# A two-layer decoder trunk on one core: rows of x loaded once, and the first half-step's instructions in a fixed order

## The chip, the core and the metric

The program runs on one core of one Trainium2 chip. The metric is the device time of one execution in microseconds. The kernel before takes 971.33 us (median of 3 runs, 970.76 to 971.44). A core has five engines with a queue of instructions each, which start in their order: TensorE (PE, with its weight loads as PEld), VectorE (DVE), ScalarE (ACT), GpSimd (POOL) and SyncE (SP, which here issues loads). They wait for each other by semaphores only.

## The reference, cut to what matters

```python
def rmsnorm(x, g):                      # x: 256 tokens x 1024, float32
    y = x * lax.rsqrt(jnp.mean(x * x, axis=-1, keepdims=True) + EPS)
    return y * g

def swiglu(x, w_gate, w_up, w_down):    # 1024 -> 2816 -> 1024
    return (jax.nn.silu(x @ w_gate) * (x @ w_up)) @ w_down

for l in range(2):
    x = x + 0.5 * swiglu(rmsnorm(x, ffn1_norm[l]), ...)      # the first half-step is this one, l = 0
    x = x + mixer(rmsnorm(x, mix_norm[l]))                   # conv and windowed attention, or block attention
    x = x + memory_cross_attention(rmsnorm(x, xa_norm[l]), mem_n, ...)
    x = x + 0.5 * swiglu(rmsnorm(x, ffn2_norm[l]), ...)
return rmsnorm(x, final_norm)
```

The change touches the start of the program and the first half-step up to about its sixth pair of gate and up columns; the arithmetic is the same.

## The kernel before, in words

x lies transposed, as eight rows of tiles `x[:, k]` (128 features by 256 tokens). Every product takes float32 apart into a high and a low part: `x2.hi` and `x2.lo` for activations, `whi` and `wlo` for weights. For one 128x128 weight tile, `mm` issues two matmuls, `whi` against both parts of x (512 columns, L391) and `wlo` against the high part (256 columns, L392). Together they are called a pair of matmuls below.

Weights come in the order of use. `Stream` loads chunks of 16 tiles (1 MB) into four `raw` buffers on SP's queue, and splits them in blocks of 8 tiles: ACT writes `whi` (L127), then DVE writes `wlo` (L128), into five buffers each. `_due_to` names how many blocks ahead of use a block may be split (`AHEAD_BLOCKS`, 4), `fill` and `flush` do it. The first 32 tiles are special: `load_first` loads one piece for each row k (L87), which holds row k of x and the four gate tiles that go with it, so x reaches the first matmuls with their weights; x is loaded a second time, whole, to the place where it stays (L1092, after a one-element copy by POOL that delays it).

The half-step computes 22 columns f of gate and of up. `gates` does the gates of f = 0 to 3 at once, row by row, as x comes in: blocks 0 to 3. Then `gate_up` does up of f = 0 to 3 (blocks 4 to 7), and from f = 4 on a gate block and an up block in turn (f = 4 is blocks 8 and 9, f = 5 is 10 and 11). A finished column is joined from its two halves in PSUM (`join`: ACT L401, then DVE L402).

1/rms is not needed for the matmuls. It comes beside them: squares on ACT and their sums on DVE (L327 to L338), a sum over features on PE (L354), the power -1/2 on POOL (L359), a transpose that spreads it over the partitions (PE L365) and a copy to `rbc` (ACT L367). Columns that are finished before that wait in a list (`n.waiting`). `evac` then takes a column f through gate times `rbc` (DVE L525), silu (ACT L526), times up (DVE L528), high part (ACT L459) and low part (DVE L460).

The order on each engine is made in two steps. `Order.run` calls the pieces by planned PE times (`pe.after(delay, ...)`), and a scheduler then may move instructions on each engine, except those that are given to `keep_in_program_order` (by `ws.pin` for splits).

Of the kernel before, what the change touches and what calls it, by code (L numbers as in the profile page):

```python
# [53 lines left out]
class Stream:  # L54
# [23 lines left out]
    def load_first(self):  # L78

        rows = []  # L80
        for k in range(KT):
            if k % 2 == 0:
                t = self.raw[k // 2] = self._raw()
            o = k % 2 * STEP
            cuts = (0, S + P, STEP) if k == 0 else (0, STEP)
# [69 lines left out]
    def take(self, name, layer, row, col, n=1, rows=1):  # L155

        i = len(self.order)
        for k in range(n):  # L160
            at = k % 2 * P
            self.order.append((name, layer, row, col + k * P, 1) if n == 1 else
                              (name, layer, row, col + 2 * at + k // 2, 2) if rows == 1 else
                              (name, layer, row + at, col + k // 2, 2))
        b, o = divmod(i, BLK)
        assert o + n <= BLK and n in (1, 4)
        self._load_to(self.chunk_of(b)[0] + 1 + self.AHEAD_CHUNKS)
        self._due_to(b + 1 + self.AHEAD_BLOCKS)
        while self.n_split <= b:
            self.fill()  # L170
        if self.part and self.n_split == b + 1 and o + n > BLK // 2:
            self.step()
        hi, lo = self.split[b]
        return hi[:, o * P:(o + n) * P], lo[:, o * P:(o + n) * P]


class Order:
# [3 lines left out]
    def __init__(self):  # L181
        self.t = 0.0
        self.tasks = []
        self.n = 0

# [57 lines left out]
def build(nc, tc, ctx, a):  # L243
# [31 lines left out]
    first_rows = ws.load_first()  # L275
# [45 lines left out]
    def squares(n, k, stream):  # L321

        if k < KT - 2:
# [3 lines left out]
            nc.scalar.activation(sq, stream[:, k - 1:k + 1].rearrange("p k s -> p (k s)"), AF.Square)  # L327
            if k == 1:
                n.acc = sq
            else:  # L330
                nc.vector.tensor_tensor(n.acc, n.acc, sq, op=ALU.add)
            if k == KT - 3:
                two, n.acc = n.acc, act.tile([P, S], F32, name="sqacc", bufs=2)
                nc.vector.tensor_tensor(n.acc, two[:, :S], two[:, S:], op=ALU.add)
# [5 lines left out]
    def norm_scale(n, delay=2300, unpin=False, wide=True, turn=True):  # L340
# [5 lines left out]
        def sums():  # L346
            pt = tr_tile()
            ms = act.tile([P, 2], F32, name="ms", bufs=2)
            for t in range(2):
                part = n.acc[:, t * P:(t + 1) * P]  # L350
                if turn:
                    nc.tensor.transpose(pt[:, t * P:(t + 1) * P], part, ident)
                else:
                    nc.tensor.matmul(pt[:, t:t + 1], part, ones, start=True, stop=True)  # L354
            if turn:
                nc.vector.tensor_reduce(ms, halves(pt[:, :S]), axis=AX.X, op=ALU.add)
            nc.vector.tensor_scalar(ms, ms if turn else pt[:, :2], 1.0 / D, EPS, op0=ALU.mult, op1=ALU.add)
            n.rcol = act.tile([P, 2], F32, name="rcolm" if n.keep else "rcol", bufs=1 if n.keep else 2)
            nc.gpsimd.tensor_tensor(n.rcol, ms, mhalf, op=ALU.pow)  # L359
            pe.after(*((2200, spread, 120) if wide else (1400, known, 0)))  # L360

        def spread():
            pt = tr_tile()
            for t in range(2):
                nc.tensor.transpose(pt[:, t * P:(t + 1) * P], n.rcol[:, t:t + 1].to_broadcast([P, P]), ident)  # L365
            n.rbc = act.tile([P, S], F32, name="rbcm" if n.keep else "rbc", bufs=1 if n.keep else 2)
            nc.scalar.activation(n.rbc, pt[:, :S], AF.Copy)  # L367
            known()

        def known():  # L370
            n.ready = True
            ws.fine = False
            if unpin:
                ws.pin = None
            for fn in n.waiting:
                fn()
# [11 lines left out]
    def mm(ps, w, x2, start, stop):  # L388


        nc.tensor.matmul(ps, w[0], x2.both, start=start, stop=False)  # L391
        nc.tensor.matmul(ps[:, :S], w[1], x2.high, start=False, stop=stop)  # L392
# [7 lines left out]
    def join(out, ps):  # L400
        nc.scalar.activation(halves(out), unpaired(ps[:, S:]), AF.Copy)  # L401
        nc.vector.tensor_tensor(halves(out), unpaired(ps[:, :S]), halves(out), op=ALU.add)  # L402
# [88 lines left out]
    def ffn(which, layer, n, nxt, first=False, last=False):  # L491
# [3 lines left out]
        def gates():  # L495
# [3 lines left out]
            for k in range(KT):  # L499
                for f in range(SIDE):  # L500
                    w = ws.take(f"{which}_w_gate", layer, k * P, f * P)
                    mm(cur[f, 0], w, n.x[k], k == 0, k == KT - 1)
            for f in range(SIDE):
                cur[f, 0] = join(w1(), cur[f, 0])

        def gate_up(f, part, ks):
            def go():
# [15 lines left out]
        def evac(f, g, u):  # L523

            nc.vector.tensor_tensor(g, g, n.rbc, op=ALU.mult)  # L525
# [5 lines left out]
            ws.flush()  # L531

# [74 lines left out]
        if first:  # L607
            for k in range(KT):
                pe.after(12000 + 1800 * (k // 2), lambda k=k: squares(n, k, x), 0)
        norm_scale(n, 18900 if first else 2300, unpin=True, turn=not first)  # L610
# [471 lines left out]
    for k in range(KT):  # L1082
# [6 lines left out]
        if k == KT // 2 - 1:  # L1089
# [122 lines left out]
```

## Time and profile before

| what | value |
|---|---|
| median of 3 runs | 971.33 us |
| the profiled execution's own time | 971.57 us |
| its span, first to last instruction | 969.8 us |
| PE busy | 959.2 us, 99% |
| DVE busy, ACT busy | 760.2 us (78%), 614.1 us (63%) |
| granted TensorE clock, mean | 0.999 |

The span leaves 1.8 us of the execution outside. Busy times are sums over the whole span; a busy PE is one with a matmul in its pipeline. The clock column of the page is in tenths of full speed and shows 9 (90% or more) in all 40 slices.

### The profile page before, as it was taken

How to read it: one execution, taken by the hardware profiler on the slowest of the kernel's cores; microseconds unless marked ns; L12 is line 12 of the kernel's file. 1: busy time of each engine (PE TensorE's matmuls, PEld its weight loads, DVE VectorE, ACT ScalarE, POOL GpSimd, SP SyncE). 2: the span in 40 equal slices, each digit the busy share in tenths (PEclk: the TensorE clock that was granted, in tenths of full speed). 3: DMA queues.
4: the chain of work that ended last, by engine and by line, in shares of the span. 5: the costliest groups of instructions: out<-in, count | busy, mean ns of one | idle time of the engine just before them, and what ended most of it. 6: DMA issues, size and time to landing. Idle time of an engine off the chain costs nothing.

```text
span 969.8 us, 16906 instructions
## 1 busy us (share of the span) xinstructions
PE 959.2 (99%) x6536; PEld 899.6 (93%) x6536; DVE 760.2 (78%) x1361; ACT 614.1 (63%) x1144; POOL 55.7 (6%) x95
## 2 busy tenths in 40 slices
PE   9999999999999999999999999999999999999997
PEld 8899999999999999999999999999999999999896
DVE  7988867898878888876778878677878789887663
ACT  7767655697657766665556666556785667666541
POOL 0410000001000000000000000000000003400011
PEclk9999999999999999999999999999999999999999
DMA  9797556555536656556555565565645346775631
GB/s 372 272 333 284 187 205 211 170 189 196 190 111 211 231 191 215 194 198 215 184 208 198 193 218 184 207 208 183 223 147 189 116 167 242 243 253 187 212 131 44
DMA packets 29921, 196.73 MB, mean 203 GB/s; under 512 B 3848, under 2 KB 4872, under 8 KB 7184
## 3 DMA queue, kind: packets, MB, share of 16 engines
q1 hardware_dynamic: 27072, 187.44, 55.5%
q0 software_dynamic: 2192, 7.37, 2.2%
q8 instruction: 51, 0.84, 0.3%
q10 hardware_dynamic: 576, 0.83, 0.2%
q14 instruction: 30, 0.25, 0.1%
HBM read 193.51 MB, written 5.27 MB: 205 GB/s over the span
## 4 chain that ended last, share of the span: by engine, by line
PE 97%; DVE 1%; DMA 1%; ACT 0%; issue 0%; SPq 0%; POOLq 0%; DVEq 0%; ACTq 0%
PE acc L391 41%; PE acc L392 21%; PE acc L397 7%; PE acc L398 7%; PE acc L396 7%; PE acc L574 1%; PE acc L573 1%; PE acc L572 1%; PE acc L918 1%; PE acc L916 1%; PE acc L917 1%; DMA raw<-in_w 1%; PE sc L572 0%; PE sc L574 0%; PE sc L573 0%; DVE wlo L128 0%
## 5 line engine op out<-in xcount | busy, mean ns | idle before, releaser
L127 ACT ACTIVATE whi<-raw 128x1024 fp32r<-128x1024 f32 (+2 forms) x377 | 369.2, 986 | 274.0 <-PE acc L391 133.3
L128 DVE TENSOR_TENSOR wlo<-raw,whi 128x1024 fp32r<-128x1024 f32 (+2 forms) x377 | 426.6, 1136 | 144.7 <-ACT whi L127 141.6
L391 PE MATMUL acc<-x,whi 128*128 128x512 f32 x1392 | 457.4, 383 | 0.9 <-DVE w L402 0.5
L392 PE MATMUL acc<-x,wlo 128*128 128x256 f32 x1392 | 377.4, 273 | 0.6 <-DVE wlo L128 0.6
L391 PEld LDWEIGHTS acc<-x,whi 128*128 128x128 f32 x1392 | 262.2, 189 | 37.4 <-ACT whi L127 1.1
L392 PEld LDWEIGHTS acc<-x,wlo 128*128 128x128 f32 x1392 | 267.2, 192 | 1.9 <-DVE wlo L128 0.9
L391 PE MATMUL acc<-h,whi 128*128 128x512 f32 x462 | 151.3, 382 | 0.0
L392 PE MATMUL acc<-h,wlo 128*128 128x256 f32 x462 | 125.4, 273 | 0.0
L391 PEld LDWEIGHTS acc<-h,whi 128*128 128x128 f32 x462 | 87.1, 189 | 12.0
L392 PEld LDWEIGHTS acc<-h,wlo 128*128 128x128 f32 x462 | 88.7, 192 | 0.2
L396 PE MATMUL acc<-h,whi 128*128 128x256 f32 x322 | 87.2, 279 | 1.6 <-ACT h L459 1.6
L397 PE MATMUL acc<-h,whi 128*128 128x256 f32 x322 | 88.1, 276 | 0.3 <-DVE h L460 0.3
L398 PE MATMUL acc<-h,wlo 128*128 128x256 f32 x322 | 87.8, 275 | 0.0
L402 DVE TENSOR_TENSOR w<-acc,w 128x256 f32<-128x256 f32 x195 | 81.1, 416 | 3.8 <-ACT w L401 3.5
L398 PE MATMUL acc<-x,wlo 128*128 128x256 f32 x304 | 83.9, 278 | 0.0
L397 PE MATMUL acc<-x,whi 128*128 128x256 f32 x304 | 83.8, 277 | 0.0
L396 PE MATMUL acc<-x,whi 128*128 128x256 f32 x304 | 83.4, 279 | 0.0
L401 ACT ACTIVATE w<-acc 128x256 f32<-128x256 f32 x195 | 71.9, 369 | 10.0 <-PE acc L392 9.8
L396 PEld LDWEIGHTS acc<-h,whi 128*128 128x128 f32 x322 | 60.5, 192 | 2.6 <-ACT h L459 2.0
L397 PEld LDWEIGHTS acc<-h,whi 128*128 128x128 f32 x322 | 61.7, 192 | 0.8 <-DVE h L460 0.7
L398 PEld LDWEIGHTS acc<-h,wlo 128*128 128x128 f32 x322 | 61.7, 192 | 0.1
L397 PEld LDWEIGHTS acc<-x,whi 128*128 128x128 f32 x304 | 58.2, 192 | 0.2
(211 smaller groups left out, 1180.7 us busy)
## 6 DMA issues: line engine op xcount, KB each, us to landing
raw<-in_w SPq DMA_DIRECT2D x171, 1024.0 KB, 5.0
dists<-line POOLq DMA_DIRECT2D x2, 1536.0 KB, 13.3
raw<-in_memT SPq DMA_DIRECT2D x3, 1024.0 KB, 5.1
raw<-in_w SPq DMA_DIRECT2D x6, 384.0 KB, 6.8
bias<-dists POOLq DMA_DIRECT2D x2, 1024.0 KB, 11.3
x<-in_xT SPq DMA_DIRECT2D x1, 1024.0 KB, 7.6
tok<-q POOLq DMA_DIRECT2D x32, 32.0 KB, 3.5
bias<-tok POOLq DMA_DIRECT2D x1, 1024.0 KB, 7.7
```

The costliest lines, as they stand in the source:

```text
L127: for ins in (self.nc.scalar.activation(hi[:, at], src, AF.Copy), self.nc.vector.tensor_tensor(lo[:, at], src, hi[:, at].bitcast(F32), op= ...
L128: self.nc.vector.tensor_tensor(lo[:, at], src, hi[:, at].bitcast(F32), op=ALU.subtract)):
L391: nc.tensor.matmul(ps, w[0], x2.both, start=start, stop=False)
L392: nc.tensor.matmul(ps[:, :S], w[1], x2.high, start=False, stop=stop)
L396: nc.tensor.matmul(ps[:, :S], w[0], x2.high, start=start, stop=False)
L397: nc.tensor.matmul(ps[:, :S], w[0], x2.low, start=False, stop=False)
L398: nc.tensor.matmul(ps[:, :S], w[1], x2.high, start=False, stop=stop)
L401: nc.scalar.activation(halves(out), unpaired(ps[:, S:]), AF.Copy)
L402: nc.vector.tensor_tensor(halves(out), unpaired(ps[:, :S]), halves(out), op=ALU.add)
L572: nc.tensor.matmul(ps, hh, wh, start=f == 0, stop=False)
L573: nc.tensor.matmul(ps, hh, wl, start=False, stop=False)
L574: nc.tensor.matmul(ps, hl, wh, start=False, stop=f == FT - 1)
```

## The change

It has five parts.

1. `load_first` loads rows 2 to 7 of x in pairs straight to where x stays, and the weights of these rows by themselves. Rows 0 and 1 still come with their weights, and once more at the end by a load of their own. The whole load of x and POOL's copy in front of it are gone.
2. From the end of the gates (`pe.kept`) until the pairs that waited for 1/rms are done, the matmuls, joins, squares, sums and splits are all given to `keep_in_program_order`.
3. Meanwhile the stream splits 2 blocks ahead of use instead of 4 (`ws.ahead`).
4. All squares go pairwise, and they stand around the joins of the gates; 1/rms is planned at 16500 instead of 18900, its spreading 2900 after it instead of 2200.
5. The waiting columns are started one each 2000 of planned time, and each goes through `evac_steps`, three steps that are 1300 apart, instead of all at once through `evac`.

The diff, cut to its core (wrapping single instructions in `keep` is shown once):

```diff
+        self.ahead = 2
...
+            if k % 2 == 0 and k > 0:
+                self.nc.sync.dma_start(x[:, k:k + 2], xT[:, k:k + 2])
+            cuts = (0, S + P, STEP) if k == 0 else (0, STEP) if k == 1 else (S, STEP)
             for i, j in zip(cuts, cuts[1:]):
                 (self.nc.scalar if k == 1 else self.nc.sync).dma_start(t[:, o + i:o + j], self.first[k][:, i:j])
-            rows.append(t[:, o:o + S])
+            rows.append(t[:, o:o + S] if k < 2 else x[:, k])
+        self.nc.sync.dma_start(x[:, :2], xT[:, :2])
...
-        self._due_to(b + 1 + self.AHEAD_BLOCKS)
+        self._due_to(b + 1 + self.ahead)
...
+    def keep(ins):
+        return tc.keep_in_program_order(ins) if pe.kept else ins
...
-        nc.tensor.matmul(ps, w[0], x2.both, start=start, stop=False)
+        keep(nc.tensor.matmul(ps, w[0], x2.both, start=start, stop=False))
...
-            for fn in n.waiting:
-                fn()
+            n.pending = len(n.waiting)
+            for i, fn in enumerate(n.waiting):
+                pe.after(i * 2000, fn, 0) if pe.kept else fn()
...
+            pe.kept, ws.pin = True, tc.keep_in_program_order
+            ws.fill()
+            for k in range(4):
+                squares(n, k, x, KT)
+            ws.fill()
             for f in range(SIDE):
                 cur[f, 0] = join(w1(), cur[f, 0])
+            ws._due_to(FIRST // BLK + 3)
+            ws.fill()
+            for k in range(4, KT):
+                squares(n, k, x, KT)
...
+        def evac_steps(f, g, u):
+            def gate():
+                keep(nc.vector.tensor_tensor(g, g, n.rbc, op=ALU.mult))
+                keep(nc.scalar.activation(g, g, AF.Silu))
+                pe.after(1300, high, 0)
+            def high():
+                keep(nc.vector.tensor_tensor(u, g, u, op=ALU.mult))
+                h[f] = h_tile()
+                keep(nc.scalar.activation(h[f].hi, halves(u), AF.Copy))
+                pe.after(1300, low, 0)
+            def low():
+                keep(nc.vector.tensor_tensor(h[f].lo, halves(u), h[f].hi.bitcast(F32), op=ALU.subtract))
+                n.pending -= 1
+                if not n.pending:
+                    pe.kept, ws.pin, ws.ahead = False, None, ws.AHEAD_BLOCKS
+            gate()
...
-        norm_scale(n, 18900 if first else 2300, unpin=True, turn=not first)
+        norm_scale(n, 16500 if first else 2300, unpin=True, turn=not first)
...
-            nc.gpsimd.tensor_copy(x[:, 0, :1], block[1][:, :1].bitcast(F32))
-            nc.sync.dma_start(x, a["xT"])
```

What this does to the engines' queues is seen at three places. The first is SP's queue at the program's start, where `raw` is a buffer for weights (384, 768 and 512 columns are pieces of the first 32 tiles, 2048 is a chunk) and DMAHW names a load that is waited for. Before:

```order
L87 DMA raw<-in_w 128x384 x2
L87 DMA raw<-in_w 128x768 x4
L87 DMA raw<-in_w 128x768 [waits DMAHW0_49]
L87 DMA raw<-in_w 128x768 [waits DMAHW1_49]
L102 DMA raw<-in_w 128x2048 [waits DMAHW3_49,DMAHW2_49,DVE_49]
L1092 DMA x<-in_xT 128x2048 [waits Pool_49]
L102 DMA raw<-in_w 128x2048 [waits DMAHW5_49,DMAHW4_49,DVE_49]
```

And in the changed kernel:

```order
L91 DMA raw<-in_w 128x384 x2
L88 DMA x<-in_xT 128x512
L91 DMA raw<-in_w 128x512 x2
L88 DMA x<-in_xT 128x512
L91 DMA raw<-in_w 128x512 [waits DMAHW0_49]
L91 DMA raw<-in_w 128x512 [waits DMAHW1_49]
L88 DMA x<-in_xT 128x512 [waits DMAHW2_49]
L91 DMA raw<-in_w 128x512 [waits DMAHW3_49]
L91 DMA raw<-in_w 128x512 [waits DMAHW4_49]
L93 DMA x<-in_xT 128x512 [waits DMAHW5_49]
L107 DMA raw<-in_w 128x2048 [waits DMAHW6_49,DVE_49]
L107 DMA raw<-in_w 128x2048 [waits DMAHW7_49,DVE_49]
```

The 1 MB load of x behind the first chunk is gone; a quarter of it, for rows 0 and 1, now stands in front of the first chunk.

The second place is ACT's queue around the copy that makes 1/rms known (`rbc`). Buffers are numbered here; of the weights' high parts, whi_405 and whi_464 are blocks 10 and 11 of the stream and whi_545 is block 12; w1_236, 239, 242 and 245 are the gates of f = 0 to 3. Before:

```order
L127 ACTIVATE whi_405<-raw_325 128x1024 [waits DMAHW7_49,DVE_49]
L127 ACTIVATE whi_464<-raw_325 128x1024 [waits DVE_49,PE_49]
L367 ACTIVATE rbc_401<-tr_398 128x256 [waits PE_49]
L127 ACTIVATE whi_545<-raw_388 128x1024 [waits DMAHW0_49,DVE_49,PE_49]
L526 ACTIVATE w1_236<-w1_236 128x256 [waits DVE_49]
L526 ACTIVATE w1_239<-w1_239 128x256 [waits DVE_49]
L526 ACTIVATE w1_242<-w1_242 128x256 [waits DVE_49]
L526 ACTIVATE w1_245<-w1_245 128x256 [waits DVE_49]
```

In the changed kernel whi_407 is block 10 and whi_437 block 11 (block 12 stands three rows below the last one here); w1_251, 254, 257 and 260 are the gates of f = 0 to 3, w1_411 and w1_441 gate and up of f = 4:

```order
L377 ACTIVATE rbc_381<-tr_378 128x256 [waits PE_49]
L564 ACTIVATE w1_251<-w1_251 128x256 [waits DVE_49]
L570 ACTIVATE h_397<-w1_294 128x2x128 [waits DVE_49]
L132 ACTIVATE whi_407<-raw_276 128x1024 [waits DMAHW1_49,Activation_49]
L412 ACTIVATE w1_411<-acc_385 128x256 [waits PE_49,Activation_49]
L564 ACTIVATE w1_254<-w1_254 128x256 [waits DVE_49]
L570 ACTIVATE h_427<-w1_318 128x2x128 [waits DVE_49]
L132 ACTIVATE whi_437<-raw_276 128x1024
L412 ACTIVATE w1_441<-acc_417 128x256 [waits PE_49,Activation_49]
L564 ACTIVATE w1_411<-w1_411 128x256 [waits DVE_49]
L564 ACTIVATE w1_257<-w1_257 128x256 [waits DVE_49]
L564 ACTIVATE w1_260<-w1_260 128x256 [waits DVE_49]
```

Before, blocks 10 and 11 are split ahead of `rbc`; now each of blocks 10 and 11 stands behind silu and high part of one waiting column, which wait for DVE.

The third place is DVE's queue at the same point, where the low parts wlo_408 and wlo_438 belong to blocks 10 and 11. The changed kernel:

```order
L563 TENSOR_TENSOR w1_251<-w1_251,rbc_381 128x256 [waits Activation_49]
L568 TENSOR_TENSOR w1_294<-w1_251,w1_294 128x256 [waits Activation_49]
L133 TENSOR_TENSOR wlo_408<-raw_276,whi_407 128x1024 [waits DMAHW1_49,Activation_49]
L413 TENSOR_TENSOR w1_411<-acc_385,w1_411 128x256 [waits DVE_49,Activation_49]
L563 TENSOR_TENSOR w1_254<-w1_254,rbc_381 128x256
L574 TENSOR_TENSOR h_397<-w1_294,h_397 128x2x128
L568 TENSOR_TENSOR w1_318<-w1_254,w1_318 128x256 [waits Activation_49]
L133 TENSOR_TENSOR wlo_438<-raw_276,whi_437 128x1024 [waits Activation_49]
```

Before, the four products with `rbc` stand together and two splits were done in front of them; now the steps of one column stand between one split and the next.

## Rows read from the trace of the kernel before

**Rows 1.** The page's first part: engine, busy us, share, instructions.

```profile
PE 959.2 (99%) x6536; PEld 899.6 (93%) x6536; DVE 760.2 (78%) x1361; ACT 614.1 (63%) x1144; POOL 55.7 (6%) x95
```

**Rows 2.** Waits of PE: line, waited for, us in total, times, longest.

```profile
PE acc L396 <- ACT h L459: 1.6, 2, 0.8
...
PE acc L392 <- DVE wlo L128: 0.6, 1, 0.6
PE acc L391 <- DVE w L402: 0.5, 1, 0.5
```

**Rows 3.** Timeline of PE: start us, us, engine, line, operation, count, idle time before.

```profile
16.95 0.37 PE L392 MATMUL acc<-x,wlo 128*128 128x256 f32 x1
...
21.86 0.61 PE L391 MATMUL acc<-x,whi 128*128 128x512 f32 x2
23.07 0.38 PE L392 MATMUL acc<-x,wlo 128*128 128x256 f32 x1 [0.60 <-DVE wlo L128]
23.28 0.38 PE L391 MATMUL acc<-x,whi 128*128 128x512 f32 x1
...
23.61 0.38 PE L391 MATMUL acc<-x,whi 128*128 128x512 f32 x1
...
39.01 0.27 PE L392 MATMUL acc<-x,wlo 128*128 128x256 f32 x1
39.78 0.45 PE L391 MATMUL acc<-x,whi 128*128 128x512 f32 x1 [0.50 <-DVE w L402]
```

**Rows 4.** Timeline of SP; last row: the load issued at 6.99, us to landing.

```profile
6.99 0.33 SPq L102 DMA_DIRECT2D raw<-in_w  x1
9.47 0.33 SPq L1092 DMA_DIRECT2D x<-in_xT  x1
...
raw<-in_w SPq DMA_DIRECT2D x1, 1024.0 KB, 7.6
```

**Rows 5.** Timeline of ACT.

```profile
14.57 2.00 ACT L127 ACTIVATE whi<-raw 128x1024 fp32r<-128x1024 f32 x2 [1.45 <-DMA raw<-in_w]
...
32.77 0.38 ACT L367 ACTIVATE rbc<-tr 128x256 f32<-128x256 f32 x1 [0.37 <-PE tr L365]
...
34.93 1.32 ACT L526 ACTIVATE w<-w 128x256 f32<-128x256 f32 x4
36.65 1.06 ACT L127 ACTIVATE whi<-raw 128x1024 fp32r<-128x1024 f32 x1 [0.40 <-PE acc L391]
37.62 0.40 ACT L459 ACTIVATE h<-w 128x256 fp32r<-128x256 f32 x1
...
41.33 0.42 ACT L526 ACTIVATE w<-w 128x256 f32<-128x256 f32 x1 [0.37 <-DVE w L525]
```

**Rows 6.** Stretches: us, busy of PE, PEld, DVE, ACT, POOL, clock, DMA share, GB/s.

```profile
8.00:10.00 2.00, 1.58 (x9) 1.50 (x10) 1.97 (x5) 2.00 (x5) 0.37 (x1) 1.00 1.03 410
...
14.00:16.00 2.00, 2.00 (x13) 1.81 (x12) 0.33 (x1) 1.43 (x2) 0.00 (x0) 1.00 1.02 426
...
36.00:40.00 4.00, 3.50 (x22) 3.00 (x21) 3.89 (x10) 3.60 (x10) 1.05 (x4) 1.00 0.56 205
```

**Rows 7.** Timeline of DVE.

```profile
15.67 2.36 DVE L128 TENSOR_TENSOR wlo<-raw,whi 128x1024 fp32r<-128x1024 f32 x2 [1.68 <-ACT whi L127]
...
33.58 1.42 DVE L525 TENSOR_TENSOR w<-w,rbc 128x256 f32<-128x256 f32 x4
...
37.74 1.23 DVE L128 TENSOR_TENSOR wlo<-raw,whi 128x1024 fp32r<-128x1024 f32 x1
38.88 0.42 DVE L460 TENSOR_TENSOR h<-w,h 128x256 fp32r<-128x256 f32 x1
39.22 0.41 DVE L402 TENSOR_TENSOR w<-acc,w 128x256 f32<-128x256 f32 x1
...
40.89 0.41 DVE L525 TENSOR_TENSOR w<-w,rbc 128x256 f32<-128x256 f32 x1
```

**Rows 8.** The spreading transposes: durations ns, first and last start us.

```profile
L365 PE MATMUL tr<-ident,rcol x2: 272/272/273, 32.4 to 32.5; 128*128 128x128 f32 x2
```

More of the change, by code (lines that the diff above doesn't have):

```diff
@@ L184, in __init__ @@
         self.n = 0
+        self.kept = False
     def after(self, delay, fn, cost):
@@ L319, in normed_tile, with squares @@
             squares(n, k, stream)
-    def squares(n, k, stream):
-        if k < KT - 2:
+    def keep(ins):
+        return tc.keep_in_program_order(ins) if pe.kept else ins
+    def squares(n, k, stream, pairs=KT - 2):
+        if k < pairs:
             if k % 2 == 0:
@@ L330, in squares @@
             else:
-                nc.vector.tensor_tensor(n.acc, n.acc, sq, op=ALU.add)
-            if k == KT - 3:
+                keep(nc.vector.tensor_tensor(n.acc, n.acc, sq, op=ALU.add))
+            if k == pairs - 1:
                 two, n.acc = n.acc, act.tile([P, S], F32, name="sqacc", bufs=2)
-                nc.vector.tensor_tensor(n.acc, two[:, :S], two[:, S:], op=ALU.add)
+                keep(nc.vector.tensor_tensor(n.acc, two[:, :S], two[:, S:], op=ALU.add))
         else:
@@ L353, in sums @@
                 else:
-                    nc.tensor.matmul(pt[:, t:t + 1], part, ones, start=True, stop=True)
+                    keep(nc.tensor.matmul(pt[:, t:t + 1], part, ones, start=True, stop=True))
             if turn:
                 nc.vector.tensor_reduce(ms, halves(pt[:, :S]), axis=AX.X, op=ALU.add)
-            nc.vector.tensor_scalar(ms, ms if turn else pt[:, :2], 1.0 / D, EPS, op0=ALU.mult, op1=ALU.add)
+            keep(nc.vector.tensor_scalar(ms, ms if turn else pt[:, :2], 1.0 / D, EPS, op0=ALU.mult, op1=ALU.add))
             n.rcol = act.tile([P, 2], F32, name="rcolm" if n.keep else "rcol", bufs=1 if n.keep else 2)
             nc.gpsimd.tensor_tensor(n.rcol, ms, mhalf, op=ALU.pow)
-            pe.after(*((2200, spread, 120) if wide else (1400, known, 0)))
+            pe.after(*((2900 if pe.kept else 2200, spread, 120) if wide else (1400, known, 0)))
         def spread():
@@ L364, in spread @@
             for t in range(2):
-                nc.tensor.transpose(pt[:, t * P:(t + 1) * P], n.rcol[:, t:t + 1].to_broadcast([P, P]), ident)
+                keep(nc.tensor.transpose(pt[:, t * P:(t + 1) * P], n.rcol[:, t:t + 1].to_broadcast([P, P]), ident))
             n.rbc = act.tile([P, S], F32, name="rbcm" if n.keep else "rbc", bufs=1 if n.keep else 2)
-            nc.scalar.activation(n.rbc, pt[:, :S], AF.Copy)
+            keep(nc.scalar.activation(n.rbc, pt[:, :S], AF.Copy))
             known()
@@ L372, in known @@
             ws.fine = False
-            if unpin:
+            if unpin and not pe.kept:
                 ws.pin = None
-            for fn in n.waiting:
-                fn()
+            n.pending = len(n.waiting)
+            for i, fn in enumerate(n.waiting):
+                pe.after(i * 2000, fn, 0) if pe.kept else fn()
             n.waiting = []
@@ L388, in mm @@
     def mm(ps, w, x2, start, stop):
-        nc.tensor.matmul(ps, w[0], x2.both, start=start, stop=False)
-        nc.tensor.matmul(ps[:, :S], w[1], x2.high, start=False, stop=stop)
+        keep(nc.tensor.matmul(ps, w[0], x2.both, start=start, stop=False))
+        keep(nc.tensor.matmul(ps[:, :S], w[1], x2.high, start=False, stop=stop))
     def mm_narrow(ps, w, x2, start, stop):
@@ L400, in join @@
     def join(out, ps):
-        nc.scalar.activation(halves(out), unpaired(ps[:, S:]), AF.Copy)
-        nc.vector.tensor_tensor(halves(out), unpaired(ps[:, :S]), halves(out), op=ALU.add)
+        keep(nc.scalar.activation(halves(out), unpaired(ps[:, S:]), AF.Copy))
+        keep(nc.vector.tensor_tensor(halves(out), unpaired(ps[:, :S]), halves(out), op=ALU.add))
         return out
@@ L514, in go @@
                 if ks[-1] == KT - 1:
+                    if pe.kept:
+                        ws.flush()
                     cur[f, part] = join(w1(), ps)
                     if part == 1:
+                        if n.ready and pe.kept:
+                            n.pending += 1
                         when_scaled(n, lambda: evac(f, cur[f, 0], cur[f, 1]))
@@ L523, in evac @@
         def evac(f, g, u):
+            if pe.kept:
+                evac_steps(f, g, u)
+                return
             nc.vector.tensor_tensor(g, g, n.rbc, op=ALU.mult)
@@ L605, in down_tok @@
                 part(range(FT - late), *right)] + [part(end, reg) for reg in right]
-        if first:
-            for k in range(KT):
-                pe.after(12000 + 1800 * (k // 2), lambda k=k: squares(n, k, x), 0)
-        norm_scale(n, 18900 if first else 2300, unpin=True, turn=not first)
+        norm_scale(n, 16500 if first else 2300, unpin=True, turn=not first)
         parts = (range(4), range(4, KT))
```

8 lines of the change are left out of this document (3 added, 5 removed).

## The prediction

> **What bounds the kernel now.** I read the busy times first, then the waits of PE, then the timelines around each wait. PE is busy 959.2 us [rows 1], so the loss is in few places. The waits of PE name them [rows 2]: 0.6 us for a `wlo` of DVE, 0.5 us for a join of DVE; the 1.6 us for ACT's h part at line 396 belong to another stage, which the change leaves alone. The timeline shows both waits in the first half-step [rows 3]. At full flow a pair of matmuls starts every 23.61 - 23.28 = 0.33 us, 0.22 for 512 columns and 0.11 for 256, so a block of eight pairs lasts 2.62 us. At 21.86 two 512-column matmuls start, and the next matmul should at 22.30; it starts at 23.07: 0.77 us lost (wait A). Behind the one at 39.01 the next should start at 39.12; it starts at 39.78: 0.66 us lost (wait B). Together 1.43 us. In 36 to 40 us, where B lies, DVE is busy 3.89 of 4.00 us and ACT 3.60 [rows 6]: there the two vector engines bound the kernel, whatever their shares of the span.
>
> The sum is made against the profiled execution, 971.57 us (a span of 969.8 and 1.8 outside); it is 0.24 above the median of the runs, 971.33, from which I count the forecast. A change under 0.2%, 1.9 us, can't be told from none.
>
> **The change, part by part.**
>
> *Loads.* The first chunk is issued at 6.99 and lands 7.6 us later [rows 4]; ACT starts on it at 14.57, having waited for it, and needs 2.00 us for two blocks [rows 5]; DVE follows at 15.67 [rows 7], PE's first matmul with a `wlo` of block 4 at 16.95 [rows 3]. The DMA engines are full all this time, 410 GB/s in 3 KB lines and 426 in 8 KB lines [rows 6], so what is queued ahead sets the landing. New ahead of the chunk is the load of x rows 0 and 1, 0.262 MB: at 410 GB/s 0.64 us. Rows 2 to 7 and their weights are the same bytes in 2 KB lines. The two rates give 3072 x 16 / 410 = 119.9 ns for a line on one of 16 engines and 307.7 ns for 8 KB, so 36.7 ns per KB and 9.8 fixed: 83.2 ns for 2 KB. 1152 such lines instead of 768 take 5.99 instead of 5.76 us, 0.23 more. The chunk lands 0.87 us later, at 15.44; whi until 16.50 (1.06) [rows 5], wlo 16.55 to 17.78, PE at 17.83: **+0.88 us**. The bounds are 0 (the small load fits beside the others) and 1.8 (the 0.87 twice). I take the sum, as this chain waits for the landing already today. The gates themselves stay ahead of their rows, since PE needs 4 x 0.33 = 1.31 us for a row, and ACT and DVE about 1 us (five instructions each from 8 to 10 us, at two a row) [rows 6]. From the second chunk on loads come earlier, 1.05 MB less 0.26 at 426 GB/s, 1.8 - 0.2 = 1.6 us; nothing waits for them then.
>
> *The pinned start.* Wait A goes: behind it stood four joins and the sums of squares on DVE, which now come after the split of block 5 or 6. **-0.77**. Between 17.8 us and the start of block 8, DVE has splits of four blocks (1.14 each from start to start), seven joins (0.34, from 38.88 to 39.22) [rows 7], three sums of 512 columns, taken as two joins each, and one of 256: 9.3 us; PE's blocks 4 to 7 last 10.5. I count no wait; it would cost some 0.3 if it appeared.
>
> *The steps of the waiting columns.* This is the large term. Let T be PE's start of the spreading transposes, now at the head of block 8. Before, blocks 10 and 11 were split ahead of `rbc`; now each stands behind the steps of one column, on ACT and on DVE. From T to the end of `rbc` it is 0.75 (32.4 to 33.15) [rows 5, 8]. A step to the other engine costs 0.03 us (DVE ends at 41.30, ACT starts at 41.33) [rows 5, 7]; I take 0.05. Block 10: gate times rbc 0.41, silu 0.42, times up 0.41, then ACT's h part, behind which `whi` can start 0.30 later, `whi` 1.06, with five steps of 0.05: 2.85. So wlo of block 10 starts at T+3.60 and ends at T+4.83; PE needs it at T + 0.25 (transposes) + 2 x 2.62 + 0.22 = T+5.71, no wait. Block 11, from one wlo start to the next: wlo 1.14, join 0.33, gate product 0.41, silu 0.42, up product 0.41, h part 0.30, whi 1.06, four steps 0.20: **4.27 us, where PE uses up a block in 2.62**. Its wlo starts at T+7.87 and ends at T+9.10; PE needs it at T+8.33: wait **0.82**. Block 12: three columns' steps stand ahead of it (f = 4, 1, 2, and f = 3 begun). Counting DVE's products one behind the other at 0.34, the high part of f = 2 starts 3.63 behind the wlo of block 11, whi 0.30 later, ending at T+12.86, while PE is there at T+11.55: wait **1.36**. The next matmul in PE's order needs whi of block 13, done 1.26 later, when PE has spent 0.22: wait **1.04**. Sum **+3.22**. Bounds: with no cost of a step and 5% shorter operations the cycle is 3.87, and the three waits come to about 2.0; below that lies only that some step isn't in the chain, down to a cycle of 2.62 and nothing; above, each step at 0.10 adds 0.2 a block, and the waits come to 3.8.
>
> *Wait B* goes with its cause, the four columns at once (DVE's row of four products at 33.58 and ACT's of silus at 34.93) [rows 5, 7]: **-0.66**.
>
> *The rest* costs nothing: POOL's copy and its wait go, the squares are one operation fewer, and they are hidden under blocks 4 to 7 as counted. Were that cover gone, it would be 0.7 on DVE per sum. From block 13 on the queues hold the same instructions in the same order, so a delay there is handed on whole: PE's 99% leaves no gap to absorb it.
>
> Sum: 0.88 - 0.77 + 3.22 - 0.66 = **+2.67 us**, 971.57 to 974.24 for an execution like the profiled one, and **974.0 us** on the median.
>
> **Where the skill would say otherwise.** In 36 to 40 us DVE has 0.11 us free of 4.00 [rows 6], beside 78% over the span [rows 1]. The Trainium skill, "Perfetto Trace Analysis", section "Identifying the Most-Contended Engine", says to find the bottleneck by occupancy and to optimise the engine with the highest. By that rule PE with 99% is the bound and an order of ACT and DVE, with 22% and more to spare, changes nothing: the third rival. The trace does not bear it out in this stage. In the longest stall of before PE's granted clock stays 1.00 (the stretch of rows 6), the level of 2.4 GHz. The Trainium skill, "TensorE: Matmul & The Clock Gate", section "HAM oscillation — how this bites in real kernels", says that idle gaps while waiting for data can drop the clock to half; that is the fourth rival, and no run here shows it.
>
> **The rivals.**
>
> 1. *Faster: the loads decide.* From the second chunk on weights land 1.6 us earlier, and if ACT and DVE then run ahead of PE so far that blocks 10 to 12 are split before PE asks, both waits go and nothing comes. For it: ACT waited 1.45 us for the first chunk [rows 5]. Against it: the splits now stand behind `rbc` in fixed queues, so earlier data can't be taken. It decides if the cycle is under 2.62 + (5.71 - 4.83) = 3.5 us. Then 0 to 0.88 - 1.43: 969.9 to 970.8 us, within 0.2% still; even both waits are less than 1.9 us. For faster than that PE would have to gain in the gates too.
> 2. *The chain is shorter than I count*, some steps overlapping, so that only block 12 is late by one wait: 0.88 - 1.43 + 1.4 = +0.9, 972.2 us. For it: DVE's rows overlap by 0.09 between neighbours [rows 7]. Against: neighbours of one chain wait for the full end.
> 3. *It is hidden*: 971.3 us, gains and losses of the size of A and B. For it the shares over the span, against it the 4.27 above.
> 4. *The clock falls* in the waits of 1.36 and 1.04 that lie close together. While at half speed a block takes 5.24 instead of 2.62 us; for one to three blocks that adds 2.6 to 7.9 to the forecast, 977 to 982 us. Against it: clock 1.00 through A and B.
>
> **How the numbers follow.** The forecast, a cycle of over 4 us, gets 0.72, with a range of its own from 972.6 (waits of 2.0, and the chunk 0.2 earlier) to 975.5 (3.8, and the chunk at 1.8). Rival 1 gets 0.08, rival 2 0.11, rival 3 0.05, rival 4 0.04. For 8 times in 10 the range is 971.9 to 975.7: the forecast's own and most of rival 2. Slower by over 0.2% means above 973.3: most of the forecast and rival 4, together 0.70. Faster by over 0.2%, below 969.4, needs rival 1 and a gain in the gates: 0.03. Within: 0.27.
>
> **What the profile after would show.** PE's wait for the first `wlo` of block 4 ends near 17.8 instead of 16.95; no wait of PE between 18 and 28; waits of PE near 37.5 (wlo) and 41 to 43 (whi, then whi or wlo), 3.2 us together; between the wlo splits of blocks 10, 11 and 12 more than 4 us from start to start, with DVE idle for ACT and ACT idle for DVE in between; no wait at 39 for a join. Without a wait near 41 the step "4.27 against 2.62" is wrong; with PE at 17.0 in block 4 the load term is; a granted clock below 1.00 near 43 would be rival 4.

## The result, and the profile after

The changed kernel takes 976.97 us (median of 6 runs, 975.97 to 979.00) against 971.38 for the kernel before in the same rounds (6 runs): a ratio of 1.0058, interval 1.0047 to 1.0070. It is slower, as forecast, but by 5.6 us and not 2.7, and outside the range I gave. The profiled execution took 977.07 us, its span 975.3.

First, where it is lost. These rows count what each engine did from the start to 50, 100 and 900 us (columns as in [rows 6]; PE first), before and then after:

```profile
0.00:50.00 50.00, 47.41 (x276) 42.67 (x277) 41.48 (x75) 37.00 (x70) 11.89 (x35) 1.00 0.84 317
0.00:100.00 100.00, 97.41 (x582) 88.64 (x583) 83.61 (x148) 70.44 (x132) 15.13 (x42) 1.00 0.85 310
0.00:900.00 900.00, 895.48 (x6169) 841.84 (x6170) 721.54 (x1309) 589.61 (x1115) 48.81 (x90) 1.00 0.60 209
```

```profile
0.00:50.00 50.00, 43.21 (x244) 38.13 (x245) 34.63 (x62) 33.26 (x62) 11.41 (x40) 1.00 0.74 261
0.00:100.00 100.00, 93.21 (x550) 84.09 (x551) 79.03 (x140) 66.89 (x125) 12.34 (x41) 1.00 0.81 292
0.00:900.00 900.00, 891.27 (x6138) 837.16 (x6139) 717.30 (x1301) 586.11 (x1108) 46.05 (x89) 1.00 0.60 207
```

At 50 us PE is 32 matmuls behind; it does 306 in the next 50 us, so that is 5.2 us. At 100 it is 32 and at 900 us 31 behind: the loss is made in the first 50 us and handed on whole.

PE's waits after, answering to [rows 2], and its timeline, answering to [rows 3]:

```profile
PE acc L402 <- ACT whi L132: 2.7, 4, 1.4
PE acc L407 <- ACT h L470: 1.6, 2, 0.8
PE acc L403 <- DVE wlo L133: 1.5, 2, 0.8
PE acc L402 <- DVE x L323: 1.4, 1, 1.4
```

```profile
10.05 0.70 PE L402 MATMUL acc<-x,whi 128*128 128x512 f32 x2 [1.45 <-DVE x L323]
...
18.53 0.48 PE L402 MATMUL acc<-x,whi 128*128 128x512 f32 x1 [0.36 <-ACT whi L132]
19.79 0.38 PE L403 MATMUL acc<-x,wlo 128*128 128x256 f32 x1 [0.78 <-DVE wlo L133]
...
38.72 0.38 PE L402 MATMUL acc<-x,whi 128*128 128x512 f32 x1
39.87 0.38 PE L403 MATMUL acc<-x,wlo 128*128 128x256 f32 x1 [0.77 <-DVE wlo L133]
...
42.27 0.27 PE L403 MATMUL acc<-x,wlo 128*128 128x256 f32 x1
43.90 0.48 PE L402 MATMUL acc<-x,whi 128*128 128x512 f32 x1 [1.36 <-ACT whi L132]
45.11 0.48 PE L402 MATMUL acc<-x,whi 128*128 128x512 f32 x1 [0.73 <-ACT whi L132]
```

Waits A and B are gone. The first `wlo` matmul of block 4 starts at 19.79 instead of 16.95: 2.84 late. Then come three new waits. By the pace of [rows 3] the matmul at 39.87 was due at 38.94, the one at 43.90 at 42.38 and the one at 45.11 at 44.12: 0.93 + 1.52 + 0.99 = 3.44 us. The sum of these four terms is 2.84 - 0.77 - 0.66 + 3.44 = 4.85 of the 5.5 us between the spans; of the 0.65 left, by the counts above, about 0.35 lies before 50 us and 0.3 behind 900, and I have no cause for them.

The gates were late, too: PE waited 1.45 us for x rows 2 and 3 at 10.05. These are the last `wlo` matmuls of the gates after, and the first matmuls of block 4 before:

```profile
17.79 0.39 PE L403 MATMUL sc<-x,wlo 128*128 128x256 f32 x2
```

```profile
16.36 0.76 PE L391 MATMUL acc<-x,whi 128*128 128x512 f32 x2
```

Two 256-column matmuls take 0.22 us, so even with the chunk in time block 4 could have begun at 18.01 at the earliest, 1.65 after the 16.36 of before. That the chunk came still later sets the 19.79.

The chain of the column steps, DVE's splits of blocks 10 to 12 and ACT between them (answering to [rows 5, 7]):

```profile
34.36 1.23 DVE L133 TENSOR_TENSOR wlo<-raw,whi 128x1024 fp32r<-128x1024 f32 x1 [1.43 <-ACT whi L132]
...
38.59 1.23 DVE L133 TENSOR_TENSOR wlo<-raw,whi 128x1024 fp32r<-128x1024 f32 x1 [1.43 <-ACT whi L132]
...
43.88 1.23 DVE L133 TENSOR_TENSOR wlo<-raw,whi 128x1024 fp32r<-128x1024 f32 x1 [1.43 <-ACT whi L132]
```

```profile
36.28 0.42 ACT L564 ACTIVATE w<-w 128x256 f32<-128x256 f32 x1 [1.69 <-DVE w L563]
37.19 0.42 ACT L570 ACTIVATE h<-w 128x256 fp32r<-128x256 f32 x1 [0.49 <-DVE w L568]
37.52 1.04 ACT L132 ACTIVATE whi<-raw 128x1024 fp32r<-128x1024 f32 x1
```

From one split to the next it is 38.59 - 34.36 = 4.23 us, then 5.29, where PE uses up a block in 2.62. DVE is idle for ACT before each split, ACT for DVE before each silu: two engines taking turns.

The loads, SP's queue (issue times, as in [rows 4]), ACT's waits for them, and the DMA rate (last column):

```profile
5.77 3.12 SPq L91 DMA_DIRECT2D raw<-in_w  x2
9.20 0.33 SPq L93 DMA_DIRECT2D x<-in_xT  x1
9.95 17.91 SPq L107 DMA_DIRECT2D raw<-in_w  x6
```

```profile
8.57 0.91 ACT L322 ACTIVATE x<-x,vecs 128x256 fp32r<-128x256 f32 x2 [1.73 <-DMA x<-in_xT]
...
17.42 1.06 ACT L132 ACTIVATE whi<-raw 128x1024 fp32r<-128x1024 f32 x1 [2.93 <-DMA raw<-in_w]
```

```profile
4.00:5.00 1.00, 1.00 (x5) 0.87 (x5) 0.52 (x2) 0.11 (x1) 0.00 (x0) 1.00 0.86 280
5.00:6.00 1.00, 0.71 (x3) 0.20 (x2) 0.04 (x1) 0.60 (x2) 0.00 (x0) 1.00 0.88 234
6.00:7.00 1.00, 1.00 (x6) 0.89 (x6) 1.00 (x3) 0.84 (x2) 0.00 (x0) 1.00 0.98 283
...
12.00:13.00 1.00, 1.00 (x9) 0.92 (x8) 1.00 (x3) 0.97 (x3) 0.00 (x0) 1.00 0.69 211
```

The first chunk is issued at 9.95 instead of 6.99 and lands at 17.42 instead of 14.57. The rate falls twice: to 234 to 283 GB/s at 4 to 7 us, where the kernel before moves 363 to 402 (its rows stand at e9), and to 211 at 12 to 13. These are the rates of all that the DMA engines moved, weights included.

The trace also has a record of each line that a DMA engine moved, and of when each of the 16 parts of a load landed, as many as there are DMA engines. In the changed kernel the median 2 KB line from 4 to 14 us took 84 ns, as priced. But of the 280 that began from 4 to 7 us, 62 took over 1.3 times the median, up to 652 ns; before, it was 16 of 367 lines of 3 KB. A load has landed with its last part. Of x rows 2 and 3 the first part is there at 5.77, 13 of 16 are at 6.93, and the last is at 8.55; ACT starts on these rows at 8.57 (row 2 before: 5.72 to 7.23). Some engines stay behind in what is queued next: the parts of the first chunk land from 15.25 to 17.40, before from 13.20 to 14.55.

### The profile page after: what moved, and what is told of

Same layout as the page of the kernel before. It is cut to its first block, busy times and chain, and to the rows that moved or that the text cites. A ratio compares the mean times of both kernels' runs of the same rounds, so it can differ in the third digit from the quotient of the medians.

```text
span 975.3 us, 16904 instructions
## 1 busy us (share of the span) xinstructions
PE 960.1 (98%) x6536; PEld 899.6 (92%) x6536; DVE 760.1 (78%) x1360; ACT 613.8 (63%) x1143; POOL 52.9 (5%) x94
## 4 chain that ended last, share of the span: by engine, by line
PE 95%; DMA 1%; DVE 1%; ACT 1%; issue 0%; SPq 0%; POOLq 0%; DVEq 0%; ACTq 0%
PE acc L402 40%; PE acc L403 20%; PE acc L408 7%; PE acc L409 7%; PE acc L407 7%; PE acc L622 1%; PE acc L621 1%; PE acc L620 1%; DMA raw<-in_w 1%; PE acc L962 1%; PE acc L961 1%; PE acc L963 1%; DMA x<-in_xT 1%; PE sc L620 0%; PE sc L622 0%
```

## The experiments

The kernel before took 971.5 to 971.7 us beside all of them. A count of PE's matmuls in the first 100 us is given as n (582 before, 550 after; 6.1 are a microsecond).

**e1_loads.** The kernel before with part 1 of the change.

> The kernel before with the change's loads alone (rows 2 to 7 of x apart, rows 0 and 1 once more, no whole load). Theory L, the loads cost as much as block 4 shows (its first wlo at PE at 19.79 us in the changed kernel, 16.95 before): the first wlo of block 4 again near 19.8, and the time 2.8 us above before, about 974.2 us (973.2 to 975.0). Theory P, that start is late because the pinned order puts something ahead of the splits: first wlo near 17.8, as I had predicted, and 972.3 us.

Measured: 972.86 us, ratio 1.0014 (1.0005 to 1.0023), n 577. The first `wlo` of block 4 on PE is at 19.57 and the chunk lands at 16.93, so the start is that of theory L, but the time is nearer to P: waits A and B are not there either. So 2.4 us of lateness cost 1.3. One reservation: without the pin the scheduler also moved ACT's and DVE's instructions, so that this is not the old order with other loads.

**e2_order.** All of the change but part 1.

```diff
-    first_rows = ws.load_first(x, a["xT"])
+    first_rows = ws.load_first()
```

> The changed kernel with the loads of before (each row of x with its weights, x whole later). Theory L: block 4 starts at 16.95 again, waits A and B stay away, the three waits of blocks 11 and 12 stay (3.4 us): +3.4 - 1.4 = +2.0, about 973.4 us (972.6 to 974.2). Theory P: block 4 near 19, and 975.5 us or more.

Measured: 977.10 us, ratio 1.0051 (1.0037 to 1.0065), n 548: as slow as the whole change, and both theories wrong. Block 4 starts at 16.95 and A and B are away, as L said. But PE waits 0.70 us for the `wlo` of block 5 and 0.43 for the sum of squares, since on DVE the squares of x, which now comes late again, stand ahead of that split. The three waits, for the `wlo` of block 11 and the `whi` of blocks 12 and 13, are the same (0.76, 1.36, 0.73), and behind them the clock falls. PE's timeline and the stretches there:

```profile
43.87 0.79 PE L398 MATMUL acc<-x,whi 128*128 128x512 f32 x1 [0.73 <-ACT whi L128]
44.46 0.42 PE L399 MATMUL acc<-x,wlo 128*128 128x256 f32 x1
44.68 0.63 PE L398 MATMUL acc<-x,whi 128*128 128x512 f32 x1
45.10 0.42 PE L399 MATMUL acc<-x,wlo 128*128 128x256 f32 x1
```

```profile
42.00:44.00 2.00, 0.61 (x2) 0.32 (x2) 1.36 (x2) 2.00 (x4) 0.00 (x0) 0.94 0.47 184
44.00:46.00 2.00, 2.00 (x7) 1.72 (x8) 2.00 (x5) 2.00 (x4) 1.72 (x5) 0.50 0.36 98
46.00:48.00 2.00, 2.00 (x10) 1.76 (x10) 2.00 (x4) 1.24 (x2) 0.60 (x2) 0.70 0.96 344
```

The granted clock is 0.50, the level of 1.2 GHz. A pair starts every 0.64 us instead of 0.33; the five pairs from 43.87 on take 3.35 us, where the same five take 1.74 in the changed kernel (45.11 to 46.85): 1.6 us lost. That is my fourth rival. In the profile of the whole change the same three waits left the clock at 1.00. The Trainium skill, "TensorE: Matmul & The Clock Gate", section "HAM oscillation — how this bites in real kernels", has waits for data drop the clock to half: this run agrees, with 0.50 behind the waits, and the profiles of the changed kernel and of e9, with 1.00 behind the same waits, do not.

**e3_ahead4** and **e4_order_ahead4.** The changed kernel, and e2, with the splits 4 blocks ahead.

```diff
-        self.ahead = 2
+        self.ahead = 4
```

> The changed kernel with the splits 4 blocks ahead instead of 2, so blocks 10 and 11 are split before rbc is copied. If the 4.2 us per block of the column steps cause the waits near 40 to 45 us (3.4 us), these go, since the steps now stand before blocks 12 to 14, which PE reaches 5.2 us later: 977.0 - 3.4 = about 973.5 us. If the waits only move to blocks 13 and 14: 976 to 977 us.

> Loads of before, the new order, splits 4 ahead: both costs taken out. If both terms add up as the traces suggest, waits A (0.77) and B (0.66) are gone and nothing comes for them: 971.4 - 1.4 = 970.0 us (969.6 to 970.8), below both kernels. If the terms don't add (a loss given back later), 971.4 or more.

Measured: 974.25 us, ratio 1.0027 (1.0017 to 1.0038), n 570; and 973.14, ratio 1.0016 (1.0007 to 1.0025), n 573. e3 lies nearer to its first theory's 973.5, 0.75 above it. The three waits are gone in both, so that the splits behind the column steps are their cause. What is left of PE's waits from 14 to 60 us, in e4:

```profile
PE tr L371 <- POOL rcol L365: 1.1, 1, 1.1
PE acc L399 <- DVE wlo L129: 0.9, 2, 0.7
PE tr L360 <- DVE sqacc L340: 0.4, 1, 0.4
```

The first is new in both: with more splits ahead of it on DVE, the mean square comes later, and POOL's power after it. So e4 misses its 970.0: beside the three waits, the order also brought those for block 5 and for the sum of squares, and the lead of 4 that takes the three away brings the one for POOL.

**e5_w_pairs, e6_x01_late, e7_split_same.** Three ways to part the number of loads from what they read: e1 with the weights of two rows by one load, e1 with rows 0 and 1 behind the first chunk, and the kernel before with four of its row loads cut in two.

```diff
# e7, against the kernel before
-            cuts = (0, S + P, STEP) if k == 0 else (0, STEP)
+            cuts = (0, S + P, STEP) if k == 0 else (0, S, STEP) if 2 <= k < 6 else (0, STEP)
```

> The kernel before with the change's loads (as the run with the loads alone), but the weights of rows 2 and 3, 4 and 5, 6 and 7 come by one load each instead of two: 10 loads ahead of the first chunk instead of 13, the same bytes in the same lines. Theory Q, the queue: only 8 loads can be under way before a load waits for the landing of the eighth before it, so 13 loads make SP issue the first chunk at 9.58 us instead of 6.99, and the DMA engines run dry. Then here the chunk is issued near 7 to 7.5, lands at 15.4 to 15.9 (with the loads alone 16.93), there is no dip of the DMA rate at 11 to 14 us, and the time is 0.3 to 1.0 below the loads alone, 971.9 to 972.6 us. Theory R, the rate: 2 KB lines and loads of x by themselves run slower (234 to 283 GB/s at 4 to 7 us against 363 to 402 before). Then the chunk lands within 0.4 us of 16.93 and the time is that of the loads alone, 972.9.

> The kernel before with the change's loads, but the second load of rows 0 and 1 of x goes behind the first chunk instead of ahead of it. 0.262 MB less in front of the chunk is 0.64 us at 410 GB/s. Theory Q: the chunk also stands one place further up among the loads that wait for a landing, so it is issued at 8.8 instead of 9.6 and lands 0.7 to 1.4 earlier than 16.93, at 15.5 to 16.2; the time is 0.3 to 1.0 below the loads alone. Theory R: 0.64 earlier at the most, 16.3 or later.

> The kernel before, with the loads of rows 2 to 5 cut in two each (x part and weights, from the same source as before, same bytes and order): 13 loads ahead of the first chunk as in the changed kernel, no load of x moved. Theory Q: the first chunk is issued near 9.5 instead of 6.99 and lands at 16 to 17 instead of 14.57; block 4 of PE is 1.5 to 2.5 later, the time 0.3 to 1.5 above before, 971.8 to 973.0. If the number of loads is harmless and the cause is where x comes from or that x is loaded again: chunk at 14.6 to 14.9 and 971.5 us.

Measured: e5 973.03 us, ratio 1.0012 (1.0003 to 1.0021); the chunk is issued at 6.94 and the DMA engines move 422 to 444 GB/s from 11 to 14 us, without the dip, as Q said; but it lands at 17.18 and the time is that of e1, as R said, with 299, 203 and 299 GB/s at 4 to 7 us. By the records of the landing, 15 of its 16 parts are there at 15.84 and the last is 1.3 us behind. e6: the chunk is issued at 8.19 and lands at 15.35, earlier than either theory had it; but 977.28 us, ratio 1.0054 (1.0041 to 1.0066). The scheduler, which is free in this kernel, ordered ACT and DVE so that `rbc` is copied at 36.16 instead of 31.80 in e1, and PE waits 3.42 us for a join at 42.60. Its time tells nothing of the loads. e7: 971.48, ratio 1.0003 (0.9994 to 1.0012), 13 loads, chunk issued at 7.13 and landed at 14.22. So the number of loads is harmless as long as they land in time. What differs is the first loads out of xT: in the kernels that take x from there in 2 KB pieces (the changed kernel, e1, e3, e5, e6, e11), 44 to 62 of 280 to 317 lines of 2 KB were slow in the sense above; in e7, where the x parts come out of w0, at most 5% were. A late issue follows where SP has to wait for the eighth load before, and without it (e5) an engine that is behind still holds back the landing.

**e8_fill_first.** e4 with blocks 4 and 5 both split ahead of the squares. Its edit also plans the spreading 3700 behind 1/rms instead of 2900, which the expectation does not say.

> Loads of before, new order, splits 4 ahead, and in addition blocks 4 and 5 are both split before the first squares and sums (in the run with the loads of before and 4 ahead PE waited 0.70 us for the low part of block 5, 0.43 for the sum of squares, 1.14 for POOL's power, since DVE first waited for x). If these three waits come from that order alone they go, DVE being 1.2 us earlier: 973.1 - 1.8 to 2.3 = 970.8 to 971.3, at or a little below before. If the rest of the order costs by itself, 972.5 or more.

Measured: 972.01 us, ratio 1.0003 (0.9994 to 1.0012). That lies between the two theories. The 0.70 went, with 0.2 of it left; the 0.4 and the 1.1 stayed. DVE's sum of squares came only 0.4 us earlier than in e4 (23.78 for 24.16), not the 1.2 counted on, so whether these two waits come from DVE's late start stays open.

**e9_x_from_w0.** The changed kernel with one source exchanged.

```diff
-                self.nc.sync.dma_start(x[:, k:k + 2], xT[:, k:k + 2])
+                self.nc.sync.dma_start(x[:, k:k + 2], self.first[k:k + 2].rearrange("k p s -> p k s")[:, :, :S])
```

> The changed kernel, but rows 2 to 7 of x are loaded from where the weights of these rows lie (w0 holds each row of x beside its weights, 3 KB lines) instead of from xT (8 KB lines, of which a load of two rows takes 2 KB pieces): same number, order and destination of the loads, 1 KB pieces. Theory X, reading 2 KB pieces out of xT is what is slow at the start: the dip of the DMA rate at 4 to 8 us (280, 234, 283, 350 GB/s in the changed kernel) goes to 340 or more, rows 2 and 3 are there before 7.8 us instead of 8.55, the first chunk lands at 16.4 or earlier instead of 17.42, and PE's first wlo matmul of block 4 starts at 18.8 or earlier instead of 19.79; the time is 975.5 to 976.5 us, as some of the gain goes into the next splits on DVE. Theory D, loads into x ahead of their weights are slow whatever they are read from: same dip, 19.5 to 19.9, 977 us.

Measured: 976.21 us, ratio 1.0046 (1.0033 to 1.0058). The same stretches as above, of the kernel before and then of e9, and what ACT and PE then do in e9:

```profile
4.00:5.00 1.00, 1.00 (x5) 0.86 (x5) 0.52 (x2) 0.31 (x2) 0.00 (x0) 1.00 0.99 373
5.00:6.00 1.00, 0.99 (x5) 0.59 (x5) 0.65 (x2) 1.00 (x3) 0.00 (x0) 1.00 1.01 363
6.00:7.00 1.00, 1.00 (x8) 0.95 (x7) 0.96 (x2) 0.24 (x1) 0.00 (x0) 1.00 1.03 402
```

```profile
4.00:5.00 1.00, 1.00 (x6) 0.85 (x5) 0.49 (x1) 0.36 (x2) 0.00 (x0) 1.00 1.02 374
5.00:6.00 1.00, 0.96 (x6) 0.67 (x5) 0.79 (x2) 1.00 (x3) 0.00 (x0) 1.00 1.07 362
6.00:7.00 1.00, 1.00 (x7) 0.91 (x7) 0.96 (x3) 1.00 (x4) 0.00 (x0) 1.00 1.04 381
```

```profile
15.17 1.06 ACT L132 ACTIVATE whi<-raw 128x1024 fp32r<-128x1024 f32 x1 [2.96 <-DMA raw<-in_w]
```

```profile
17.54 0.38 PE L403 MATMUL acc<-x,wlo 128*128 128x256 f32 x1 [0.78 <-DVE wlo L133]
```

Theory X: the first dip is gone, SP issues the chunk at 7.35, it lands at 15.17, and block 4 starts at 17.54. All 2.25 us of it show in the profiled execution (974.86 against 977.07) but only 0.8 in the median, where the two intervals overlap. Few lines are slow here from 4 to 7 us (5% or less, of the 1 KB and of the 2 KB lines), and the parts of the chunk land from 14.25 to 15.15. The slowest execution, 977.21 us, had a mean clock of 0.996 against 0.999; which part of the untraced executions' time is clock can't be told without their traces.

**e11_ahead_after_ms, e10_x_early, e12_x_early_15.** The changed kernel with 4 ahead from the mean square on; that with x from w0, rows 0 and 1 copied by POOL, and squares and two splits ahead of the joins; and the latter with 1/rms planned earlier.

```diff
# e11; e10 and e12 too
+            if pe.kept:
+                ws.ahead = ws.AHEAD_BLOCKS
```

> The changed kernel with the splits 2 blocks ahead only until the mean square is computed, then 4 ahead. With 4 ahead from the start PE waited 1.14 us for POOL's power, since the mean square stood behind two more splits on DVE. If that is all that is left of the order's cost, the three waits of blocks 11 and 12 (3.4 us) go and this one does not come: 977.0 - 3.4 = 973.6, below the 974.25 of 4 ahead from the start; 973.0 to 973.8 us. If the waits for the splits come back: 975 or more.

> A version meant to keep what the change gains: x from w0 for rows 2 to 7, rows 0 and 1 copied on the chip by POOL instead of loaded again, all squares ahead of the split of block 4 (x is there by then), splits of blocks 4 and 5 ahead of the joins, 4 ahead once the mean square is computed. If the two causes found are the whole loss (the landing of the first chunk, the splits behind the column steps), block 4 starts at 17.0 to 17.8 and no wait follows up to 50 us: 971.5 + 0.4 - 1.4 = 970.4 us (969.8 to 971.2), below both kernels. If not, 971.5 or more, with a wait that the profile names.

> As the version with x early, with 1/rms planned 1500 earlier (15000 instead of 16500), so that the spreading transposes stand half a column or a block earlier on PE and fewer columns wait for them. If 1/rms is not what PE waits for there, the same time within 0.3 us; if the copies and sums are then too late for it, PE waits at the transposes, 0.5 to 1.5 us more.

Measured: e11 973.66 us, ratio 1.0020 (1.0011 to 1.0029), as expected: neither the three waits nor the 1.1 (one of 0.31 for a join is left). So the column steps were worth 3.3 us in the medians. e10 971.76, ratio 1.0003 (0.9994 to 1.0012), n 587: with both causes taken out, and squares and sums moved besides, the time is back to that of before, not below it at 970.4 as the first theory had it. Its profiled execution is 0.5 shorter (971.09), with one wait left, 1.14 us for the `wlo` of block 4 at 17.47. e12 972.36, ratio 1.0007 (0.9998 to 1.0016): no difference from e10 that these intervals show.

**e13_x_early_halves, e14_before_halves.** e10, and the kernel before, with the first chunk loaded as two halves.

> The version with x early, with the first chunk loaded as two halves of 512 KB (block 4 is the first half). PE waited 1.14 us there for the low part of block 4, at 17.47 us. If that wait is for the bytes of the chunk, the first half lands 512 KB / 420 GB/s = 1.2 us earlier, the wait goes and the time is 0.8 to 1.1 below the version with x early, 970.7 to 971.0 us, below both kernels. If the wait is for ACT and DVE, which square and sum x ahead of the split, the same time, 971.8.

> The kernel before with the first chunk loaded as two halves of 512 KB, and nothing else. ACT waited 1.45 us for the chunk there and PE's first wlo matmul of block 4 started at 16.95. If PE was waiting for the landing, block 4 starts up to 1.2 us earlier, near 15.8; the time falls by 0 to 1.2 us, as the wait for the next splits (0.77 at 23) may grow by what is won: 970.4 to 971.6 us. If the landing of the chunk did not decide, 971.6.

Measured: 971.40 us, ratio 0.9999 (0.9991 to 1.0008), and 971.43, ratio 1.0000 (0.9991 to 1.0009): no gain in either. In e14 ACT starts on block 4 at 13.04 instead of 14.57, and PE then waits at 22.16 and 23.10 (0.72, 0.46) for the splits of blocks 6 and 7, the next chunk: what is won at block 4 is handed back two blocks later. In e13 the landing did not decide: ACT is busy with the squares until it starts on block 4 at 15.57, without a wait for a load. No version here beats the kernel before.

**e15_x_one_load.** The changed kernel with rows 2 to 7 by one load, in 6 KB pieces.

> The changed kernel, but rows 2 to 7 of x come by one load (6 KB pieces of the 8 KB rows of xT) where rows 2 and 3 were loaded. The gates of rows 2 to 7 wait for all of x, so this is not for the time (977 to 979 us) but for the rate. Theory S, small pieces out of xT are slow: with 6 KB pieces the rate at 4 to 8 us is 370 GB/s or more. Theory T, xT is slow in the first microseconds whatever the piece: again 200 to 350 GB/s there.

Measured: 978.93 us, ratio 1.0076 (1.0062 to 1.0089); 416, 362, 334 and 363 GB/s at 4 to 8 us, nearer to S. But 21 of its 125 lines of 6 KB took over 1.3 times their median, up to 912 ns, and of the 16 parts of rows 2 to 7 fifteen are there at 7.08 and the last at 8.31. So lines out of xT are often slow here, too, and a length of 2 KB is not the reason alone. PE, which waited 3.21 us for x at 11.42, has a granted clock of 0.50 behind that wait, and again behind the three later ones:

```profile
14.00:16.00 2.00, 2.00 (x8) 1.72 (x7) 1.10 (x2) 0.31 (x1) 0.00 (x0) 0.50 0.81 328
...
48.00:50.00 2.00, 2.00 (x9) 1.72 (x8) 2.00 (x3) 2.00 (x5) 1.23 (x4) 0.50 0.98 264
```

## Why the prediction was wrong, step by step

- **Loads, +0.88: the step that failed.** "The DMA engines are full all this time" and "so what is queued ahead sets the landing" put the chunk at 15.44 and block 4 at 17.83. Measured: 17.42 and 19.79, +2.84, beyond my upper bound of 1.8 too. The price of a line came out (84 ns for 83.2). What was wrong is that every engine would be as fast as the bytes ahead of it: 62 of 280 lines were slow, the rate was 234 to 283 GB/s, each load landed with its slowest engine, and SP, waiting for the eighth load before, could not issue the chunk before 9.95. The same paragraph let the gates "stay ahead of their rows"; PE waited 1.45 us for rows 2 and 3. With the same loads from w0 (e9) the step holds: 15.17 and 17.54. So the exchange of the source, 2 KB pieces of xT for 1 KB pieces of w0, is what made the difference; why lines out of xT are so often slow in the first microseconds stays open. The lateness also differs between executions: with the same loads as in the changed kernel the chunk landed at 16.93, 16.51 and 16.20 in e1, e3 and e11.
- **The chain, +3.22: right**, in mechanism, place and size: 4.23 us a block against 4.27 forecast, 3.44 lost. e3, e4 and e11 take it away, e2 keeps it. It comes 2.4 us later than I said (39.87 for 37.5); of that, 1.96 is block 4's own lateness (19.79 for 17.83).
- **Waits A and B, -1.43:** gone, but the credit was not the order's alone: they are gone with the loads alone, too (e1).
- **"I count no wait" in blocks 4 to 8:** true of the changed kernel, and of e9 with the chunk at 15.17. With the loads of before (e2), where ACT's squares wait for x until 17.12, 0.70 + 0.43 us appear, where I had priced 0.3.
- **Rival 3, all hidden,** is out. The Trainium skill, "Perfetto Trace Analysis", section "Identifying the Most-Contended Engine", goes by the highest occupancy, and for TensorE by its weight loads' busy share; with PEld at 93% [rows 1] that points to PE. The trace does not agree in this stage: PE's waits ended with VectorE and ScalarE, at 78% and 63% of the span.
- **Rival 4, the clock,** I gave 0.04. It is not in the changed kernel's profile, but in those of e2, at half the clock behind the same waits, and of e15. It deserved more than 0.04, as a part of the forecast, since it can follow from the waits that I forecast.
- **The sum:** of the 2.8 us between 2.67 and the span's 5.5, the loads are 1.96, the chain 0.22, and 0.65 stays open.
- **Two slips that change nothing.** The two line rates give 37.6 ns per KB and 7.2 fixed, so 82.3 ns for 2 KB instead of 83.2. The clock of 1.00 that I put down to the longest stall stands in the stretch of wait B, not of A; in that of A, 22 to 24 us, it is 1.00 as well.

## What to carry to other kernels

A load lands with its slowest engine, and an engine that falls behind stays behind through the loads queued next. So the median price of a line does not tell when a load lands; where a load reads from a new place and no row of the trace shows its own lines, the bounds must be wide. An order laid down by hand that puts two engines in turns costs the whole cycle per block, and giving the splits two blocks more of a lead takes it away. A gain ahead of a loaded stage is easily handed back there (what e14 won at block 4 was lost at block 6), so what a fix is worth is read behind the stage, by the count of matmuls done.

## What the runs showed of the hardware

In the first microseconds of the program, from 4 to 7 us, lines that came out of xT were often slow: where 2 KB pieces of its 8 KB rows were loaded (the changed kernel, e1, e3, e5, e6, e11), 14 to 22% of the 2 KB lines, which here are x and weights together, took over 1.3 times the median, and with 6 KB pieces (e15) 17% of those. With the rows of x out of w0, it was 5% or less of the 1 KB and 2 KB lines (e7, e9, e10, e12, e13), and 8% or less of the 3 KB lines (before, e2, e4, e8, e14). From 7 to 11 us it was 13 of 751 lines of 2 KB in the changed kernel. It is not the first microseconds alone: in e9, whose rows 0 and 1 still come out of xT, 34 of 71 such lines were slow from 11 to 14 us. Why, no run here shows; 1 KB pieces out of xT were not tried.

The median line moved at nearly one rate whatever its length: 1 KB in 46 ns, 2 KB in 84, 6 KB in 234 and 8 KB in 309, which is 22 to 27 bytes per ns. The Trainium skill, "DMA: Bandwidth & Descriptors", section "Specifications", gives 512 B as the least transfer for line rate; the trace agrees for these medians, while the slow lines, of 2 and 6 KB alike, are another matter.

The clock fell to half behind two waits of 1.36 and 0.73 us in one profile (e2) and stayed full behind the same two in others (the changed kernel, e9: 1.40 and 0.73). What decides between them stays open.
